# Forgetting attention: transposes of large tiles in a pair of PSUM banks, split by one pass per engine

## The chip, the cores and the metric

The kernel runs on one core of a Trainium2 chip. The metric is the device time of one execution in microseconds (us). Three runs of the kernel before gave 2591.21, 2593.04 and 2594.58 us; the median is 2593.04 us.

Engine names are those of the profile: PE is TensorE, PEld its weight loads, DVE is VectorE, ACT is ScalarE, POOL is GpSimd, SP is SyncE. Each engine runs its own instructions in the order of the program and waits on semaphores for the others.

## What is computed

The program is three transformer layers in fp32 over 1024 tokens of width 1024: a first block (two kinds of attention and a mixture of experts), then a layer with forgetting attention, then a layer with windowed attention. The change lies in the forgetting attention alone:

```python
def fox_attention(q, k, v, log_f):                 # 16 heads, head size 64, 1024 tokens
    c = jnp.cumsum(log_f, axis=1)
    ...
    def block(args):                               # one block of 128 queries
        idx, qi, ci = args
        logits = jnp.einsum('bqhd,bkhd->bhqk', qi, k) * scale
        logits = logits + ci[..., :, None] - c_k[..., None, :]
        logits = jnp.where(causal, logits, -jnp.inf)
        p = jax.nn.softmax(logits, axis=-1)
        return jnp.einsum('bhqk,bkhd->bqhd', p.astype(v.dtype), v)
```

## The kernel before

`phase_fox` works through 16 heads. A head has eight tiles of 128 queries, `qt` 0 to 7; tile `qt` looks at `qt + 1` blocks of 128 keys. The order within a head is 7, 0, 6, 1 and then 5, 2, 4, 3, so that a large tile (`qt` 4 to 7, 5 to 8 blocks, at even `i`) and a small one (`qt` 0 to 3, 1 to 4 blocks, at odd `i`) alternate. The generator `unit(h, half, i)` is one tile, 128 in all. It is cut by `yield` into steps; `go.feed` takes every tile that is under way one step further, the oldest first, and then starts the next one. So in one feed stand, in this order: the last step of tile u-3, the second step of tile u-1, the first step of tile u. The order on each engine is the order in which these steps are written.

1. First step: two or four matmuls of queries and keys (L2117, L2118) into `p_s0` or `p_s1`, then DVE adds the mask and the forget terms and takes the row minimum (L2123).
2. Second step: ACT takes the exponential and the row sum (L2131), from SBUF to SBUF.
3. Last step: PE transposes the tile block by block into PSUM (L2148), `split` copies it out on ACT (rounded to the fast fp32 format, the high part, L341) and DVE subtracts this from the PSUM tile (the low part, L342). The matmuls with the values (L2054, L2055) read both parts three feeds later.

PSUM has eight banks of 512 fp32 columns. In this phase `p_s0` has banks 0 and 1, `p_s1` bank 2, `p_pv` banks 3 and 7. The transposes take their banks from `p_tr`, a ring of banks 4, 5 and 6 that is used all over the program: each call of `tile` takes the next bank. A large tile takes two (four blocks in the first, the rest in the second) and has one `split` for each; a small tile takes one.

After every second head, `scaled(j)` (L2075) makes the factors that normalize a pair of heads: DVE takes the reciprocal of the row sums (L2078), PE transposes it (L2081), ACT copies it out (L315 through `acopy`), and it goes through DRAM (`d_ra`) to all partitions. It is started when the pair's last tile, `qt` 3, takes its second step. Its PE transpose is written right behind the transposes of that `qt` 3 tile and takes the next bank of `p_tr`. A wait is made for whoever last read or wrote the bank's place.

Of the kernel before, what the change touches and what calls it, by code (L numbers as in the profile page):

```python
# [19 lines left out]
P = 128  # L20
# [45 lines left out]
def f(ap):  # L66
    return ap.bitcast(F32)
# [226 lines left out]
def three_layer_kernel(ctx: ExitStack, tc: tile.TileContext, I, out, stop=99, dbg=None):  # L294
    nc = tc.nc
    V, A, G, T, SP = (GUARD(e) for e in (nc.vector, nc.scalar, nc.gpsimd, nc.tensor, nc.sync))
    ctx.enter_context(tc.manual_schedule())
    sb = Arena(ctx.enter_context(tc.tile_pool(name="sbuf", bufs=1)), SLOTS, SMALL)
    banks = Banks(ctx.enter_context(tc.tile_pool(name="psum", bufs=1, space=PSUM)).tile([P, 4096], F32, name="ps"))
    p_mm = banks.ring([0], [1], [2], [3])  # L300
    p_s = banks.ring([0, 1], [2, 3])
    p_tr = banks.ring([4], [5], [6])
# [34 lines left out]
    def split(hi, lo, src, scale=None, e=V):  # L337

        if scale is None:
            if e is V:  # L340
                A.activation(out=hi, in_=src, func=AF.Copy)  # L341
                e.tensor_tensor(lo, src, f(hi), op=OP.subtract)  # L342
            else:
                e.tensor_copy(hi, src)
                for k in range(src.shape[1]):
                    fine(lo[:, k], src[:, k], f(hi[:, k]), OP.subtract)
        else:
            A.activation(out=hi, in_=src, func=AF.Copy, scale=scale)
            V.scalar_tensor_tensor(lo, src, scale, f(hi), op0=OP.mult, op1=OP.subtract)
# [1664 lines left out]
    def phase_fox(og, wo, last):  # L2014

        p_s0, p_s1, p_pv = banks.ring([0, 1]), banks.ring([2]), banks.ring([3], [7])
        fc, pp, ptp, sm = Rings(sb), Rings(sb, 2), Rings(sb, 2), Rings(sb, 4)
        CS, cs = {}, fc.tile([P, 10 * P], F32, name="cs")

        def masked(h, qt):  # L2020


            c = FX[h][2]
            n = (qt + 1) * P
            if qt > 3:
                d = slice(qt * P, n)
                G.affine_select(out=c[:, d], in_=c[:, d], compare_op=OP.is_ge, fill=-BIG, base=0, pattern=[[-1, P]],
                                channel_multiplier=1)
                CS[qt] = c[:, :n]
            else:  # L2030
                CS[qt] = cs[:, qt * (qt + 1) // 2 * P:][:, :n]
                G.affine_select(out=CS[qt], in_=c[:, :n], compare_op=OP.is_ge, fill=-BIG, base=qt * P,
                                pattern=[[-1, n]], channel_multiplier=1)

        pp.reserve_pairs("sb", 2)
        pp.reserve_pairs("pt", 4)
        RS, PT, ended, late = {}, {}, set(), []
        todo = Todo(FDELAY)


        ORDER = ((7, 0, 6, 1), (5, 2, 4, 3))

        def pv_chunks(h, top, hi, lo):

            v = FX[h][3]
            box = {}

            def chunk(k0, k1):
                if k0 == 0:
                    box["ps"] = p_pv.tile([P, 256], name="pv")  # L2050
                ps = box["ps"]
                for kt in range(k0, k1):
                    q0 = P if kt == top else 0
                    T.matmul(ps[:, q0:], lhsT=v[:, kt], rhs=hi[:, kt, q0:], start=(kt == 0), stop=False)  # L2054
                    T.matmul(ps[:, q0:], lhsT=v[:, kt], rhs=lo[:, kt, q0:], start=False, stop=(kt == top))  # L2055
                if k1 == top + 1:
                    a = h % 2 * 64
                    o = og.at(h // 2, top - 1, 2)[a:a + 64]
                    acopy(o, ps[0:64])
                    late.append((o, ps[64:128], h, top))  # L2060
                    if top == 3:
                        sb.drop(f"fv{h}")

            for k0 in range(0, top + 1, 2):
                todo.add(lambda k0=k0: chunk(k0, k0 + 2))

        def add_halves():

            for o, ps, h, top in late:
                V.tensor_tensor(o, o, ps, op=OP.add)  # L2070
                if top == 3:
                    ended.add(h)
            late.clear()

        def scaled(j):  # L2075

            r = RS.pop(j)
            V.reciprocal(r, r)  # L2078
            yield
            ps = p_tr.tile([P, 4, P], name="rtr")[0:16, 0]  # L2080
            T.transpose(ps, r.rearrange("p a t -> p (a t)"), ident)  # L2081
            rt = sm.tile([16, P], F32, name="rt")
            acopy(rt, ps)
            yield
            yield
            SP.dma_start(out=d_ra[2 * j:2 * j + 2].rearrange("a (t p) -> (a t) p", p=P), in_=rt)
            yield
            yield
            rr = pp.tile([P, S], F32, name="rr")
            for a in range(2):  # L2090
                bc_load(rr[a * 64:(a + 1) * 64], d_ra[2 * j + a], S)
            yield
            yield
            while 2 * j + 1 not in ended:
                yield
            for th in range(2):
                o = og.at(j, 4 * th, 4)
                fine(o, o, rr[:, th * 512:(th + 1) * 512], OP.mult)

        def unit(h, half, i):  # L2100
            todo.step()
            qt = ORDER[half][i]
            if half == 0 and i == 0:
                if h % 2 == 0:
                    RS[h // 2] = sm.tile([P, 2, NT], F32, name="rs")
            if half == 0 and i == 3:
                fox_load(h + 1)
            if half == 1 and i == 2:
                fox_load_v(h + 1)
            q, k, c = FX[h][:3]  # L2110
            qs = slice(qt * P, (qt + 1) * P)
            n = (qt + 1) * P
            todo.some(FTAKE)
            ps = (p_s1 if i % 2 else p_s0).tile([P, 512 if i % 2 else S], name="s")
            for c0 in range(0, n, 512):
                w = min(512, n - c0)
                T.matmul(ps[:, c0:c0 + w], lhsT=q[:, qs], rhs=k[:, 0, c0:c0 + w], start=True, stop=False)  # L2117
                T.matmul(ps[:, c0:c0 + w], lhsT=q[:, qs], rhs=k[:, 1, c0:c0 + w], start=False, stop=True)  # L2118
            nm = sm.tile([P, 1], F32, name="nm")
            sbt = pp.tile([P, S], F32, name="sb")  # L2120
            pt = pp.tile([P, S], F32, name="pt", bufs=4)

            V.tensor_tensor_reduce(sbt[:, :n], ps[:, :n], CS[qt], -1.0, 3e38, OP.add, OP.min, nm)  # L2123
            add_halves()
            if half == 1 and i == 3:
                sb.drop(f"fq{h}", f"fk{h}", f"fc{h}")
            u = 8 * h + 4 * half + i + 2
            if u < 128:
                masked(u // 8, ORDER[u // 4 % 2][u % 4])
            yield  # L2130
            A.activation(out=pt[:, :n], in_=sbt[:, :n], func=AF.Exp, scale=-1.0, bias=nm,  # L2131
                         accum_out=RS[h // 2][:, h % 2, qt:qt + 1])
            if half == 1 and i == 3 and h % 2:
                go.spawn(scaled(h // 2))
            yield
            yield
            kind = i % 2
            if i < 2:
                nb = (8, 4)[kind]
                PT[h, half, kind] = (ptp.tile([P, nb, 256], F32R, name=f"phi{kind}"),  # L2140
                                     ptp.tile([P, nb, 256], F32R, name=f"plo{kind}"))
            hi, lo = PT[h, half, kind]
            cs = slice((qt % 2) * P, (qt % 2 + 1) * P)
            for b in range(0, qt + 1, 4):
                m = min(4, qt + 1 - b)
                tr = p_tr.tile([P, 4, P], name="ptr")
                for j in range(m):
                    T.transpose(tr[:, j], pt[:, (b + j) * P:(b + j + 1) * P], ident)  # L2148
                split(hi[:, b:b + m, cs], lo[:, b:b + m, cs], tr[:, :m])
            if i >= 2:  # L2150
                pv_chunks(h, qt | 1, hi, lo)

        masked(0, 7)
        masked(0, 0)
        for h in range(16):
            for half in range(2):
                for i in range(4):
                    wo.step(WO_FOX.get(8 * h + 4 * half + i, ()))
                    go.feed(unit(h, half, i))
        last()  # L2160
        n = 0
        while go.active or go.fresh or not todo.empty():
            todo.step()
            todo.some(3)
            go.feed()
            add_halves()
            if n == 0:
                pp.drop("sb")
            if n == 2:
                pp.drop("pt")  # L2170
            wo.step(WO_FOX.get(128 + n, ()))
            n += 1
        for r in (fc, pp, ptp, sm):
            r.close()
# [345 lines left out]
```

## Time and profile before

| | |
|---|---|
| median of three runs | 2593.04 us |
| the profiled execution's own time | 2593.18 us |
| span of its profile, first to last instruction | 2591.4 us |
| PE / DVE / ACT busy over the span | 94% / 70% / 56% |
| forgetting attention | about 1780 to 2024 us of the span |
| mean granted TensorE clock | 0.973 of full speed |

A busy share over the whole span mixes stages with different limits; for this change only the stretch of the forgetting attention counts. A matmul's end is modelled in the profile, and matmuls overlap, so that consecutive ones start closer together than each one takes. In a timeline row stand the start in us from the span's start, the duration, engine, line, operation, tiles, size and count; the bracket at its end is the idle time of the engine before it and what ended it.

### The profile page before, as it was taken

Reading aid. Unit: us, or ns where it says so; the run is one execution under the profiler, and the core shown is the slowest. Engines: PE = TensorE matmul, PEld = TensorE weight load, DVE = VectorE, ACT = ScalarE, POOL = GpSimd, SP = SyncE. Lnnn points to the kernel's source line nnn. Section 1 sums busy time; section 2 is a strip of 40 time slices with the busy share of each in tenths; the row PEclk is TensorE's granted clock in tenths of the full one; section 3 lists DMA queues with packets and bytes.
Section 4 is the critical chain, followed back from the end, with each engine's and each line's share of the span. In section 5 each row is a group of like instructions: output and inputs, shape, how many; then the busy total and the mean of one; then the engine's idle time right before and its main releaser. Section 6 shows DMA issues by size and latency. Waiting matters only on the chain. (4 is left out here: it accounts for less than half of the span.)

```text
span 2591.4 us, 36430 instructions
## 1 busy us (share of the span) xinstructions
PE 2424.8 (94%) x12998; PEld 1987.6 (77%) x12998; DVE 1825.9 (70%) x3051; ACT 1439.2 (56%) x2513; POOL 648.8 (25%) x714
## 2 busy tenths in 40 slices
PE   5999899998988999999996999999999899999989
PEld 3889788887876777777765978787888689787867
DVE  7654588887667999999998445535998546655952
ACT  3324577777216888888874434324888334424940
POOL 0000089936001222222211022201234102210340
PEclk9999999999988999999998999999999899999989
DMA  7346765553748999999978544336776436336833
GB/s 266 116 130 174 226 190 166 172 172 119 254 176 275 385 390 387 384 378 381 382 280 283 174 127 122 113 103 176 192 211 193 148 110 181 108 110 168 228 104 124
DMA packets 300237, 542.70 MB, mean 209 GB/s; under 512 B 45307, under 2 KB 206331, under 8 KB 273430
## 3 DMA queue, kind: packets, MB, share of 16 engines
q1 hardware_dynamic: 292886, 523.56, 62.1%
q0 software_dynamic: 7168, 16.79, 1.9%
q8 instruction: 104, 1.70, 0.3%
q14 instruction: 79, 0.65, 0.1%
HBM read 434.68 MB, written 113.98 MB: 212 GB/s over the span
## 5 line engine op out<-in xcount | busy, mean ns | idle before, releaser
L365 PE MATMUL ps<-t,t 128*128 128x512 f32 (+4 forms) x8224 | 1761.6, 371 | 20.6 <-ACT t L341 15.6
L365 PEld LDWEIGHTS ps<-t,t 128*128 128x128 f32 (+1 forms) x8224 | 1374.2, 183 | 338.6 <-ACT t L341 17.1
L342 DVE TENSOR_TENSOR t<-t,t 128x2048 fp32r<-128x2048 f32 (+4 forms) x258 | 494.0, 1942 | 57.8 <-ACT t L341 57.5
L341 ACT ACTIVATE t<-t 128x2048 fp32r<-128x2048 f32 (+4 forms) x258 | 420.2, 1632 | 157.6 <-PE ps L365 115.9
L342 DVE TENSOR_TENSOR t<-ps,t 128x512 fp32r<-128x512 f32 (+3 forms) x628 | 371.1, 620 | 56.0 <-ACT t L341 52.8
L341 ACT ACTIVATE t<-ps 128x512 fp32r<-128x512 f32 (+3 forms) x628 | 316.1, 539 | 166.1 <-PE ps L377 70.4
L322 POOL TENSOR_TENSOR small<-small 128x8 f32<-128x8 f32 (+3 forms) x120 | 137.6, 1147 | 899.4 <-DVE small L321 861.9
L335 POOL TENSOR_TENSOR t<-t,t 128x256 f32<-128x256 f32 (+1 forms) x288 | 212.3, 770 | 118.1 <-DMA t<-d_rb 31.0
L317 ACT ACTIVATE t<-ps,small 96x512 f32<-96x512 f32 (+3 forms) x168 | 104.4, 621 | 202.8 <-PE ps L365 200.0
L315 ACT ACTIVATE t<-ps 64x256 f32<-64x256 f32 (+5 forms) x200 | 83.6, 420 | 130.3 <-PE ps L365 69.8
L1572 POOL DMA_INDIRECT d_ye<-t,small x32 | 45.2, 1412 | 437.0 <-ACT t L317 430.3
L2131 ACT ACTIVATE t<-t,small 128x1024 f32<-128x1024 f32 (+7 forms) x128 | 99.1, 775 | 27.4 <-DVE small L2123 24.3
L2123 DVE CUSTOM_DVE_ANT_0 t<-ps,t 128x1024 f32<-128x1024 f32 (+7 forms) x128 | 95.7, 747 | 23.1 <-PE ps L2118 13.2
L377 PE MATMUL ps<-small,t 96*128 96x96 f32 (+1 forms) x608 | 76.3, 264 | 35.0 <-DVE t L1930 18.7
L377 PEld LDWEIGHTS ps<-small,t 96*128 96x128 f32 (+1 forms) x608 | 67.5, 145 | 52.8 <-DVE t L1930 19.1
L453 DVE TENSOR_TENSOR t<-ps,t 128x512 f32<-128x512 f32 x32 | 22.1, 691 | 113.2 <-PE ps L365 102.3
L686 POOL TENSOR_SCALAR t<-t,small 128x1024 f32<-128x1024 f32 x32 | 93.1, 2910 | 32.6 <-DMA t<-in_w_ada_dram 32.6
L2227 DVE TENSOR_TENSOR t<-t,ps 128x512 f32<-128x512 f32 x32 | 22.0, 687 | 110.5 <-PE ps L365 110.5
L1568 POOL DMA_INDIRECT t<-d_h,small x32 | 89.0, 2783 | 37.7 <-DVE small L1276 28.2
L1769 DVE TENSOR_REDUCE small<-t 128x8 f32<-128x512 f32 (+1 forms) x56 | 36.2, 647 | 85.7 <-ACT t L1768 85.5
L2148 PE MATMUL ps<-small,t 128*128 128x128 f32 x576 | 89.3, 282 | 5.8 <-ACT t L2131 3.5
L1150 PE MATMUL ps<-t,t 128*128 128x512 f32 x320 | 83.4, 407 | 7.8 <-ACT t L1196 7.5
(297 smaller groups left out, 2984.5 us busy)
## 6 DMA issues: line engine op xcount, KB each, us to landing
t<-in_w_expert_gate_dram SPq DMA_DIRECT2D x64, 1024.0 KB, 10.7
t<-in_w_expert_up_dram SPq DMA_DIRECT2D x64, 1024.0 KB, 10.8
t<-in_w_expert_down_dram SPq DMA_DIRECT2D x64, 1024.0 KB, 10.1
t<-in_w_ada_dram SPq DMA_DIRECT2D x48, 512.0 KB, 5.1
t<-d_ak SPq DMA_DIRECT2D x64, 256.0 KB, 6.9
t<-in_w_in_a_dram SPq DMA_DIRECT2D x14, 1024.0 KB, 7.7
t<-in_x_dram SPq DMA_DIRECT2D x16, 512.0 KB, 5.2
t<-d_dk SPq DMA_DIRECT2D x16, 512.0 KB, 8.5
```

The lines of the kernel that those rows point to most:

```text
L317: A.activation(out=dst, in_=src, func=AF.Copy, scale=scale)
L322: G.tensor_tensor(dst, dst, mhalf[:, :dst.shape[-1]], op=OP.pow)
L335: G.tensor_tensor(out[:, c:c + 256], a[:, c:c + 256], b[:, c:c + 256], op=op)
L341: A.activation(out=hi, in_=src, func=AF.Copy)
L342: e.tensor_tensor(lo, src, f(hi), op=OP.subtract)
L365: T.matmul(ps, lhsT=a(k), rhs=b(k), start=(first and i == 0), stop=(last and i == n - 1))
L377: T.transpose(ps[:, k], src[:, (c + k) * P:(c + k + 1) * P], ident[:m, :m])
L686: G.tensor_scalar(w, w, cc[:, k:k + 1], None, op0=OP.mult)
L1568: G.indirect_dma_start(out=xg[e % 3], out_offset=None, in_=d_h2, in_offset=rows(idx_in[:CAP, e:e + 1]), bounds_check=S - 1, oob_is_err=False)
L2123: V.tensor_tensor_reduce(sbt[:, :n], ps[:, :n], CS[qt], -1.0, 3e38, OP.add, OP.min, nm)
L2131: A.activation(out=pt[:, :n], in_=sbt[:, :n], func=AF.Exp, scale=-1.0, bias=nm, accum_out=RS[h // 2][:, h % 2, qt:qt + 1])
L2148: T.transpose(tr[:, j], pt[:, (b + j) * P:(b + j + 1) * P], ident)
```

## The change

Within `phase_fox` the transposes no longer use `p_tr`. Large tiles write all their blocks into one tile of two banks, 4 and 5 (`p_t0`), and small tiles into bank 6 (`p_t1`). A tile of either kind is split by one ACT copy and one DVE subtraction over all its blocks; the small tiles had one of each before. The transpose of the reciprocal row sums in `scaled` takes bank 6 as well.

```diff
         p_s0, p_s1, p_pv = banks.ring([0, 1]), banks.ring([2]), banks.ring([3], [7])
+        p_t0, p_t1 = banks.ring([4, 5]), banks.ring([6])
...
-            ps = p_tr.tile([P, 4, P], name="rtr")[0:16, 0]
+            ps = p_t1.tile([P, 4, P], name="rtr")[0:16, 0]
             T.transpose(ps, r.rearrange("p a t -> p (a t)"), ident)
...
-            for b in range(0, qt + 1, 4):
-                m = min(4, qt + 1 - b)
-                tr = p_tr.tile([P, 4, P], name="ptr")
-                for j in range(m):
-                    T.transpose(tr[:, j], pt[:, (b + j) * P:(b + j + 1) * P], ident)
-                split(hi[:, b:b + m, cs], lo[:, b:b + m, cs], tr[:, :m])
+            m = qt + 1
+            tr = p_t1.tile([P, 4, P], name="ptr") if kind else p_t0.tile([P, 8, P], name="ptr")
+            for j in range(m):
+                T.transpose(tr[:, j], pt[:, j * P:(j + 1) * P], ident)
+            split(hi[:, :m, cs], lo[:, :m, cs], tr[:, :m])
```

Lines of the changed kernel behind the new ring are one higher up to L2144 (L2081 is L2082, L2117 is L2118); the transposes stay on L2148.

PE, kernel before, where the third pair of heads begins: the last tile of the head before (`qt` 3, four blocks), the transpose of the reciprocals, the matmuls of the new head's `qt` 6 and the transposes of its `qt` 7.

```order
L2148 MATMUL ps<-small,t_13152 128x128 [waits DVE_49,Activation_49]
L2148 MATMUL ps<-small,t_13152 128x128 x3
L2081 MATMUL ps<-small 16x128 [waits DVE_49]
L2117 MATMUL ps<-t_13740,t_13051 128x512
L2118 MATMUL ps<-t_13740,t_13051 128x512
L2117 MATMUL ps<-t_13740,t_13051 128x384
L2118 MATMUL ps<-t_13740,t_13051 128x384
L2148 MATMUL ps<-small,t_13151 128x128 [waits Activation_49]
L2148 MATMUL ps<-small,t_13151 128x128 x3
L2148 MATMUL ps<-small,t_13151 128x128 [waits DVE_49]
L2148 MATMUL ps<-small,t_13151 128x128 x3
```

The same place on PE in the changed kernel, with the values' matmuls left out, up to the transpose of the next small tile (`qt` 0, one block).

```order
L2148 MATMUL ps<-small,t_13152 128x128 [waits DVE_49,Activation_49]
L2148 MATMUL ps<-small,t_13152 128x128 x3
L2082 MATMUL ps<-small 16x128 [waits DVE_49]
L2118 MATMUL ps<-t_13714,t_13051 128x512
L2119 MATMUL ps<-t_13714,t_13051 128x512
L2118 MATMUL ps<-t_13714,t_13051 128x384
L2119 MATMUL ps<-t_13714,t_13051 128x384
L2148 MATMUL ps<-small,t_13151 128x128 [waits Activation_49]
L2148 MATMUL ps<-small,t_13151 128x128 x7
...
L2148 MATMUL ps<-small,t_13151 128x128 [waits Activation_49]
```

The transposes keep their place; the eight blocks of `qt` 7 have one wait in front instead of two, and the transpose of the reciprocals now stands directly behind four transposes into the same bank 6. The `qt` 0 transpose writes this bank again, and it has no wait for DVE any more: what it would wait for, the subtraction that reads the `qt` 3 tile, is covered by an earlier wait on PE.

DVE, kernel before, at the same place: from the low part of `qt` 4 (two subtractions) over the reciprocal to the low part of `qt` 3.

```order
L342 TENSOR_TENSOR t_13192<-ps,t_13190 128x4x128 [waits Activation_49]
L342 TENSOR_TENSOR t_13192<-ps,t_13190 128x128 [waits Activation_49]
L2078 RECIPROCAL small<-small 128x16
L2123 ISA t_13150,small<-ps,t_13149 128x128 [waits DVE_49,PE_49,Pool_49]
L2123 ISA small 128x1
L2070 TENSOR_TENSOR t_13145<-t_13145,ps 64x256 [waits Activation_49]
L342 TENSOR_TENSOR t_13223<-ps,t_13222 128x4x128 [waits Activation_49]
```

DVE in the changed kernel, the same stretch.

```order
L342 TENSOR_TENSOR t_13192<-ps,t_13190 128x5x128 [waits Activation_49]
L2079 RECIPROCAL small<-small 128x16
L2124 ISA t_13150,small<-ps,t_13149 128x128 [waits DVE_49,PE_49,Pool_49]
L2124 ISA small 128x1
L2071 TENSOR_TENSOR t_13145<-t_13145,ps 64x256 [waits Activation_49]
L342 TENSOR_TENSOR t_13221<-ps,t_13220 128x4x128 [waits Activation_49]
```

The low part of `qt` 4 is one subtraction over five blocks; the rest keeps its order: the reciprocal stands four instructions ahead of the subtraction that reads the `qt` 3 tile.

## Rows read from the trace of the kernel before

**Rows 1.** Windows: the whole forgetting attention, and two neighbouring heads; columns as headed.
```profile
core 0: us, PE busy (x) PEld busy (x) DVE busy (x) ACT busy (x) POOL busy (x), PEclk, DMA share, GB/s
1780.00:2024.00 244.00, 220.52 (x1586) 199.26 (x1587) 212.31 (x519) 205.32 (x518) 78.42 (x174) 0.98 0.75 201
1852.46:1866.45 13.99, 13.46 (x102) 12.34 (x101) 13.22 (x32) 12.57 (x34) 3.81 (x10) 1.00 0.78 194
1866.45:1881.46 15.01, 13.69 (x103) 12.39 (x102) 13.43 (x33) 13.19 (x32) 3.12 (x9) 1.00 0.74 186
```

**Rows 2.** Waits in 1780 to 2024 us: total, times, longest us.
```profile
PE ps L2081 <- DVE small L2078: 10.2, 8, 1.3
```

**Rows 3.** Timeline where a head begins and the reciprocals are transposed.
```profile
1867.34 0.62 PE L2148 MATMUL ps<-small,t 128*128 128x128 f32 x4
...
1867.78 1.15 ACT L2131 ACTIVATE t<-t,small 128x1024 f32<-128x1024 f32 x1
...
1868.96 0.24 DVE L2078 RECIPROCAL small<-small 128x16 f32<-128x16 f32 x1
...
1869.26 0.28 PE L2081 MATMUL ps<-small 128*16 128x128 f32 x1 [1.30 <-DVE small L2078]
...
1869.45 0.60 ACT L341 ACTIVATE t<-ps 128x512 fp32r<-128x512 f32 x1
...
1870.08 0.69 DVE L342 TENSOR_TENSOR t<-ps,t 128x512 fp32r<-128x512 f32 x1 [0.20 <-ACT t L341]
...
1870.20 1.28 PE L2148 MATMUL ps<-small,t 128*128 128x128 f32 x8
```

**Rows 4.** Chain of waits, last TensorE piece before the next head's first DVE instruction.
```profile
1881.09 0.25 PE ps L2118
```

**Rows 5.** Timeline, same head: the tile `qt` 6, then the transposes of `qt` 5.
```profile
1874.25 0.93 PE L2148 MATMUL ps<-small,t 128*128 128x128 f32 x7
...
1874.89 0.98 ACT L341 ACTIVATE t<-ps 128x512 fp32r<-128x512 f32 x2 [0.48 <-PE ps L2148]
...
1876.02 1.16 DVE L342 TENSOR_TENSOR t<-ps,t 128x512 fp32r<-128x512 f32 x2
...
1876.86 0.85 PE L2148 MATMUL ps<-small,t 128*128 128x128 f32 x6
```

**Rows 6.** Timeline, the head before it: the same two tiles.
```profile
1858.96 0.93 PE L2148 MATMUL ps<-small,t 128*128 128x128 f32 x7
...
1859.91 0.95 ACT L341 ACTIVATE t<-ps 128x512 fp32r<-128x512 f32 x2
...
1860.72 1.15 DVE L342 TENSOR_TENSOR t<-ps,t 128x512 fp32r<-128x512 f32 x2
...
1861.83 0.87 PE L2148 MATMUL ps<-small,t 128*128 128x128 f32 x6 [0.28 <-ACT t L2131]
```

**Rows 7.** Groups by form, 1780 to 2024 us: busy, mean ns, idle before.
```profile
L342 DVE TENSOR_TENSOR t<-ps,t 128x512 fp32r<-128x512 f32 x96 | 64.7, 687 | 3.6 <-ACT t L341 2.1
...
L342 DVE TENSOR_TENSOR t<-ps,t 128x256 fp32r<-128x256 f32 x32 | 13.4, 419 | 0.5
```

**Rows 8.** Timeline: two DVE subtractions of one large tile (`qt` 7).
```profile
1857.42 1.28 DVE L342 TENSOR_TENSOR t<-ps,t 128x512 fp32r<-128x512 f32 x2
```

**Rows 9.** Timeline of PE: two waits elsewhere in the program.
```profile
1531.88 0.60 PE L1901 MATMUL ps<-small 128*16 128x128 f32 x4 [2.51 <-DVE t L1902]
...
541.45 0.47 PE L1187 MATMUL ps<-t,t 128*128 128x512 f32 x1 [3.00 <-DMA t<-d_dq]
```

**Rows 10.** Windows of 20 us around those two waits and around Rows 3.
```profile
1526.00:1546.00 20.00, 17.49 (x80) 14.00 (x80) 7.50 (x13) 3.86 (x8) 4.75 (x3) 0.91 0.29 79
...
535.00:555.00 20.00, 16.89 (x111) 15.02 (x110) 15.37 (x25) 13.29 (x29) 7.34 (x6) 1.00 0.78 251
...
1864.00:1884.00 20.00, 18.52 (x136) 16.56 (x134) 17.91 (x44) 17.71 (x44) 5.66 (x13) 1.00 0.75 198
```

**Rows 11.** Timeline at the phase's end: last `qt` 3 subtraction, last transpose of reciprocals.
```profile
2023.39 0.63 DVE L342 TENSOR_TENSOR t<-ps,t 128x512 fp32r<-128x512 f32 x1
...
2023.52 0.28 PE L2081 MATMUL ps<-small 128*16 128x128 f32 x1 [1.11 <-DVE small L2078]
```

## The prediction

> **What bounds the kernel now.** I read the busy shares by window first, since the shares over the whole span mix stages. In the 244 us of the forgetting attention PE is busy 221, DVE 212 and ACT 205 us [rows 1]: three engines near 90% on one loop, each waiting briefly for the others, so the end is set by a chain that passes from engine to engine. The loop repeats every two heads, 14.0 + 15.0 = 29.0 us, although both heads have the same work; in the second PE is idle more. The waits say where: PE stands 10.2 us in total, eight times, up to 1.3 us, before the transpose of the reciprocals [rows 2], once per pair. The timeline of one such place shows the order of things [rows 3]: the four transposes of the old head's `qt` 3 end at 1867.96, the reciprocal at 1869.20, PE goes on at 1869.26, 0.06 us later, the price of a signal from DVE to PE. From there the chain of waits, read forward, names almost only TensorE until the next head's first DVE instruction, its last piece being the query-key matmul at 1881.09 to 1881.34 [rows 4]. So in this head whatever delays that transpose delays the head's end.
>
> **What the change saves.** Each of the 64 large tiles loses one ACT and one DVE instruction. The DVE subtraction takes 687 ns at 512 columns and 419 at 256 [rows 7], 1.05 ns per column and 0.15 us fixed. Two back to back overlap: 1.28 us for the pair [rows 8], against 0.687 + 512 x 1.05 = 1.22 for one of 1024 columns. The saving is 0.06 us, 64 x 0.06 = 3.8 us of DVE, and about as much of ACT. At most this reaches the end, at least nothing. I count no separate gain: the saved time is in the durations that I use below.
>
> The Trainium skill, page "VectorE: DVE Perf Modes", section "The TRN2 errata", puts the fixed cost of one DVE instruction at about 150 cycles measured; that would be an estimated 0.156 us for each instruction left out, 10 us for 64. The trace agrees on the size of the fixed part, but shows that a neighbour hides most of it; the pair's measured 1.28 us decides.
>
> **The transpose of the reciprocals.** Before, it takes the next bank of the ring, and waits for the reciprocal alone. Now it writes bank 6, into which PE has just put the four blocks of `qt` 3. It may not start until ACT has copied these out and DVE has subtracted. The printed order bears this out: the next small tile's transpose into that bank lists no wait for DVE any more, so an earlier one covers it. That subtraction cannot come sooner: ACT is first held by the 1.15 us exponential of the new head's `qt` 7 and an output copy, and copies `qt` 3 only at 1869.45 to 1870.05; DVE subtracts at 1870.08 to 1870.77 [rows 3]. With 0.06 for the signal PE goes on at 1870.83, not 1869.26: +1.57 us. The bounds are 0 (it still goes with the reciprocal) and 1.57; the rows leave nothing in between, and I take 1.57. Queued behind it on PE are the matmuls of `qt` 6, for which DVE waits, and the transposes of `qt` 7; behind the copy of the reciprocals on ACT stands the exponential of `qt` 0, which has slack.
>
> Something goes in exchange. The eight transposes of `qt` 7 took 1.28 us [rows 3]; seven take 0.93 [rows 5] and four 0.62 [rows 3], 0.10 each, so eight take 1.04 to 1.09. The rest was a wait in the middle, for the same `qt` 3 subtraction, whose bank the ring had given to their second half. That wait is now behind: -0.2 us. Net +1.37 per pair.
>
> **The later start of the copy.** ACT could begin after four transposes, now it needs all. Where this matters is `qt` 6 followed by `qt` 5, whose transposes write the same two banks and now wait for one undivided subtraction. In the head with the reciprocals [rows 5], shifted by 1.37: the transposes of `qt` 6 run 1875.62 to 1876.55, the copy of 896 columns (0.91, the pair's 0.98 less 0.07) ends at about 1877.50, the subtraction (1.09) at 1878.62, and with the signal `qt` 5 starts at 1878.68 in place of 1876.86: +1.82, so another 0.45. In the other head [rows 6]: the transposes end at 1859.89, the copy at 1860.83, the subtraction, which before ran beside the second copy from 1860.72 on, from 1860.86 to 1861.95, and `qt` 5 starts at 1862.01 in place of 1861.83: +0.18. The bounds of this term are 0 and 0.63 per pair; the durations are those of the rows, and I take 0.63. For `qt` 7 I count nothing: its subtraction waits behind another DVE instruction anyway, and the copy's end comes before; that cover is some 0.2 us thick. For `qt` 5 and 4 the passes are shorter.
>
> Sum per pair 2.0 us. Seven pairs follow each other: 14.0 us. The eighth transpose of reciprocals, at the phase's end, waits until 2024.02 + 0.06 in place of 2023.52 [rows 11], up to +0.55 on the way to the next layer, at least 0 since ACT and DVE are busy with weights there; I take 0.3.
>
> **The clock of TensorE.** The wait at each pair grows from 1.30 to about 1867.96 to 1870.83 = 2.87 us. The seven waits of 1.30 us leave the clock at full speed (1.00 over the 20 us around one [rows 10]). Longer ones often do not: after the wait of 2.51 us at 1531.88 [rows 9] the mean over 20 us is 0.91 [rows 10], which is 0.09 x 20 = 1.8 us of full-speed time gone; after 3.00 us at 541.45 it stays 1.00. In the trace there are six such waits of 2.0 to 3.0 us standing alone, of which these two are shown; after five the clock fell to its lower level, 1.2 in place of 2.4 GHz. PE has no slack in the 12 us behind the reciprocals, so a fall there costs all of about 1.7 us. Bounds: none to seven falls, 0 to 12 us. By the share seen, 5 of 6, I take five: 8.5 us.
>
> The Trainium skill ("TensorE: Matmul & The Clock Gate", Part 1) states that the clock is at one of two levels and that an idle TensorE is throttled; by that rule the longer wait is what speaks most against this change. The five falls agree with it, the wait of 3.00 us shows an exception.
>
> **The sum.** 2593.2 (profiled execution, 0.14 above the median, so I use it for both) + 14.0 + 0.3 + 8.5 = 2616.0 us.
>
> **Rivals.**
> The bank makes PE wait, but the clock holds: 2593.2 + 14.3 = 2607.5 us, and 2602.8 if only the 1.37 per pair arrives. For it: the 3.00 us wait without a fall. Against: the other five.
>
> The shorter passes win. DVE and ACT together set the pace in the first head of the pair, and if PE's wait at the reciprocals costs less than 3.8 / 7 = 0.5 us per pair, the saving of up to 3.8 us decides: 2589.4 us. For it: DVE busy 13.2 of 14.0 us there [rows 1]. Against: the wait is on PE, in order, and PE's chain behind it has no gap to take it up; and the saving is already spent on the later start of the copy.
>
> Both cancel, or the transpose of the reciprocals does not wait for the subtraction after all: 2593 us. Against: the missing DVE wait in the printed order.
>
> The two banks lock all large tiles: transposes, copy and subtraction in a ring with one buffer. For `qt` 7 that is 1.04 + 1.01 + 1.22 + 0.15 for signals = 3.4 us, against 3.5 to 3.75 us for a large and a small tile (14.0 / 4, 15.0 / 4). It fits by a hair; if the queues in front of ACT and DVE add 0.3 us on the 32 tiles of `qt` 7 and 6, 10 us come on top of the forecast: 2626 us.
>
> **How the numbers follow.** Forecast with falls of the clock: 0.58, its own range 2610 to 2621 us (two to seven falls). Bank wait without falls: 0.27. Locked large tiles: 0.06. Cancelling: 0.05. Faster: 0.04. The range 2602 to 2622 takes in the first two with the bounds of their terms; outside remain the last three, 0.15. A measurement of this kernel can tell 0.2%, 5.2 us, from no change: faster means under 2587.9, slower over 2598.2. The first three cases are slower, 0.91; cancelling is same, 0.05; faster 0.04.
>
> **What would show it.** In the profile after: the wait of PE before the transpose of the reciprocals is about 2.9 us, eight times in all, with the subtraction (L342) as what ended it; a pair of heads takes about 31 us without and 32.7 with a fall; the clock row shows falls behind these waits; in the matmul's waits the large transposes appear as waiting for DVE L342. The copies of large tiles number 64 and take about 1.0 us at 1024 columns. Wrong would be the forecast if the transpose of reciprocals is still released by the reciprocal, if PE's chain behind it has gaps that shrink, or if the seven longer waits leave the clock at 1.00 throughout.

## The result, and the profile after

The changed kernel takes 2615.78 us in the median of four runs (2612.31 to 2619.97), the kernel before 2593.70 us (2591.21 to 2594.58). The ratio is 1.0089, with a 95% interval of 1.0077 to 1.0101: slower by 0.9%. The profiled execution took 2616.51 us, its span is 2614.8 us.

The waits of the forgetting attention name the place. PE waits as often as before for the transpose of the reciprocals (L2082 now), eight times, but seven of these waits are 2.86 us long instead of 1.30 (the eighth, at the phase's end, 1.59 instead of 1.11), and something else ends the wait: VectorE's subtraction L342, not the reciprocal [rows 2]. Columns are total, times and longest wait in us.

```profile
PE ps L2082 <- DVE t L342: 21.6, 8, 2.9
```

The timeline of one such place, the start of the same head as in [rows 3], with start, duration, operation and the idle time before it:

```profile
1868.57 0.62 PE L2148 MATMUL ps<-small,t 128*128 128x128 f32 x4
...
1869.01 1.15 ACT L2132 ACTIVATE t<-t,small 128x1024 f32<-128x1024 f32 x1 [0.17 <-DVE small L2124]
...
1870.13 0.24 DVE L2079 RECIPROCAL small<-small 128x16 f32<-128x16 f32 x1
...
1870.68 0.60 ACT L341 ACTIVATE t<-ps 128x512 fp32r<-128x512 f32 x1
...
1871.31 0.69 DVE L342 TENSOR_TENSOR t<-ps,t 128x512 fp32r<-128x512 f32 x1 [0.20 <-ACT t L341]
...
1872.05 0.28 PE L2082 MATMUL ps<-small 128*16 128x128 f32 x1 [2.86 <-DVE t L342]
...
1872.99 1.79 PE L2148 MATMUL ps<-small,t 128*128 128x128 f32 x8
```

The reciprocal is there at 1870.37, but PE starts 0.05 us after the subtraction has ended, at 1872.00. The eight transposes of `qt` 7 take 1.79 us without a wait inside: here the clock falls (0.60 from 1873.0 to 1873.5). Windows from one transpose of reciprocals to the next (that is one pair of heads) show both parts of the loss side by side. The columns are those of [rows 1].

```profile
1840.86:1872.05 31.19, 26.87 (x201) 24.74 (x201) 26.34 (x57) 25.66 (x57) 8.32 (x20) 1.00 0.72 187
1872.05:1904.79 32.74, 28.46 (x202) 26.31 (x203) 26.34 (x57) 25.74 (x57) 8.35 (x20) 0.93 0.69 178
1904.79:1938.75 33.96, 29.66 (x201) 27.24 (x201) 26.43 (x57) 25.64 (x57) 8.31 (x20) 0.90 0.67 170
```

Before, a pair took 29.0 us [rows 1]. At full clock (1.00) it now takes 31.19, that is 2.19 more; where the clock falls, 32.74 and 33.96. DVE's and ACT's busy time does not move, so they only wait longer. Windows of 20 us around the seven places have clocks of 1.00, 1.00, 0.91, 0.83, 0.83, 0.91 and 0.91; two of them:

```profile
1861.00:1881.00 20.00, 16.57 (x112) 15.24 (x111) 14.63 (x33) 14.68 (x32) 4.02 (x12) 0.91 0.66 163
1892.00:1912.00 20.00, 16.58 (x106) 15.28 (x105) 14.31 (x33) 14.40 (x35) 2.74 (x8) 0.83 0.62 162
```

So the clock fell behind five of seven waits of 2.86 us, behind none of the seven of 1.30 us before (one of them in [rows 10]). The late copies stand in the same head, to be held against [rows 5]:

```profile
1878.38 0.93 PE L2148 MATMUL ps<-small,t 128*128 128x128 f32 x7
...
1879.34 0.92 ACT L341 ACTIVATE t<-ps 128x896 fp32r<-128x896 f32 x1 [0.80 <-PE ps L2148]
...
1880.29 1.09 DVE L342 TENSOR_TENSOR t<-ps,t 128x896 fp32r<-128x896 f32 x1 [0.18 <-ACT t L341]
...
1881.53 0.85 PE L2148 MATMUL ps<-small,t 128*128 128x128 f32 x6 [0.54 <-DVE t L342]
```

ACT idles until the seventh transpose has ended, DVE until the whole copy has, and PE 0.54 us until the subtraction has. Before, the copy started after four transposes, and PE did not wait here.

The transposes of `qt` 7, then `qt` 6 and `qt` 5 of both heads, in the pair of heads from 1840.86 on in which the clock does not fall:

```profile
1841.80 1.04 PE L2148 MATMUL ps<-small,t 128*128 128x128 f32 x8
...
1845.62 0.93 PE L2148 MATMUL ps<-small,t 128*128 128x128 f32 x7
...
1848.80 0.85 PE L2148 MATMUL ps<-small,t 128*128 128x128 f32 x6 [0.59 <-DVE t L342]
...
1859.93 0.93 PE L2148 MATMUL ps<-small,t 128*128 128x128 f32 x7
...
1863.09 0.85 PE L2148 MATMUL ps<-small,t 128*128 128x128 f32 x6 [0.56 <-ACT t L315]
```

From the start of `qt` 6 to that of `qt` 5 it is 3.18 and 3.16 us, against 2.60 and 2.87 at the same places before: 0.58 and 0.29 more. The eight transposes of `qt` 7 take 1.04 us instead of the 1.28 of [rows 3], since there is no wait inside. Together with the longer wait for the reciprocals' place, 1.56 - 0.24 + 0.58 + 0.29 = 2.19 us: the pair's loss at full clock comes apart without a rest. In the second head the profile names an output copy (L315) as what ended the wait, but the subtraction of `qt` 6 ends 0.15 us before the transposes start, as in the first head, and it, not L315, reads the banks that they write.

The single pass itself is as cheap as reckoned: 1024 columns take 1221 ns on DVE, against 1.28 us for the pair of halves [rows 8].

```profile
L342 DVE TENSOR_TENSOR t<-ps,t 128x1024 fp32r<-128x1024 f32 x16 | 19.5, 1221 | 9.8 <-ACT t L341 9.8
...
L341 ACT ACTIVATE t<-ps 128x1024 fp32r<-128x1024 f32 x16 | 16.4, 1025 | 14.5 <-PE ps L2148 13.8
```

### The profile page after: what moved, and what is told of

It is laid out like the page before. It is cut to its first block, busy times and chain, and to the rows that moved or that the text cites. A ratio compares the mean times of both kernels' runs of the same rounds, so it can differ in the third digit from the quotient of the medians.

```text
span 2614.8 us, 36288 instructions
## 1 busy us (share of the span) xinstructions
PE 2422.4 (93%) x12998; PEld 1986.7 (76%) x12998; DVE 1823.2 (70%) x2987; ACT 1438.2 (55%) x2449; POOL 648.7 (25%) x714
## 5 line engine op out<-in xcount | busy, mean ns | idle before, releaser
L342 DVE TENSOR_TENSOR t<-t,t 128x2048 fp32r<-128x2048 f32 (+4 forms) x258 | 493.1, 1938 | 57.4 <-ACT t L341 57.1
L342 DVE TENSOR_TENSOR t<-ps,t 128x512 fp32r<-128x512 f32 (+7 forms) x564 | 366.8, 673 | 69.7 <-ACT t L341 67.2
L341 ACT ACTIVATE t<-ps 128x512 fp32r<-128x512 f32 (+7 forms) x564 | 311.9, 583 | 185.5 <-PE ps L377 69.8
L315 ACT ACTIVATE t<-ps 64x256 f32<-64x256 f32 (+5 forms) x200 | 83.5, 419 | 130.6 <-PE ps L365 69.8
L2148 PE MATMUL ps<-small,t 128*128 128x128 f32 x576 | 89.7, 286 | 14.1 <-DVE t L342 5.3
L453 DVE TENSOR_TENSOR t<-ps,t 128x512 f32<-128x512 f32 x32 | 22.1, 691 | 113.2 <-PE ps L365 102.6
L455 ACT ACTIVATE t<-t 128x512 f32<-128x512 f32 x32 | 20.2, 632 | 125.5 <-DVE t L453 125.5
```

Source lines behind the costliest of these rows:

```text
L2148: T.transpose(tr[:, j], pt[:, j * P:(j + 1) * P], ident)
```

## The experiments

The theory: the loss is the wait on the shared bank 6, the falls of the clock behind it, and, smaller, the late pass (the one copy and one subtraction of a large tile, which start only when all its blocks are transposed). The chief rival: the pair of banks with its one buffer, and the passes over it, hold up all large tiles.

**e1_pair: the change, with the transpose of the reciprocals in the pair of banks.**

```diff
-            ps = p_t1.tile([P, 4, P], name="rtr")[0:16, 0]
+            ps = p_t0.tile([P, 8, P], name="rtr")[0:16, 0]
```

> The changed kernel, with the transpose of the reciprocals in the pair of banks 4 and 5 instead of bank 6. Those are free once the subtraction of the tile of qt 4 has ended, about 0.2 us before the reciprocal. Theory (the shared bank 6 and the clock falls behind it make the loss): TensorE again waits 1.3 us for the reciprocal, the clock stays at full speed behind the seven places, and only the later start of the copies is left, 0.4 to 0.7 us per pair of heads: 2595 to 2599 us. Rival (the large tiles lock in their one buffer): the time stays over 2605 us with the 1.3 us wait. Rival (shorter passes would win without the wait): 2589 us.

Measured: 2599.12 us, 1.0020 of the kernel before (1.0010 to 1.0030). That is just above the range expected. With this one edit some 17 of the 22 us are gone. The wait is short again, and the reciprocal ends it; a pair of heads takes 29.73 us at full clock:

```profile
PE ps L2082 <- DVE small L2079: 9.7, 8, 1.2
```

```profile
1842.02:1871.75 29.73, 27.03 (x202) 24.69 (x202) 26.31 (x58) 25.50 (x58) 8.29 (x20) 1.00 0.77 197
```

The large tiles still share one buffer and one pass, so the locking of all large tiles is not the main cause. What remains is 0.73 us per pair over the 29.0 of [rows 1].

**e2_samebank: the kernel before, with that transpose in the bank of the `qt` 3 tile.**

```diff
+            p_tr.i -= 1
             ps = p_tr.tile([P, 4, P], name="rtr")[0:16, 0]
```

> The kernel before, with one edit: the transpose of the reciprocals goes into the bank of the qt 3 tile just transposed. Rings, passes and copies are those of before. Theory: TensorE waits 2.86 us at each pair, released by the subtraction, +1.37 us per pair, 9.6 us in all, and about five falls of the clock for 8.5 us more: 2611 us (2603 to 2616). Rival (one pass over two banks and the later copy make the loss): no change, 2594 us.

Measured: 2609.94 us, 1.0066 (1.0045 to 1.0088). The bank alone, without any change to the passes, brings most of the loss. The wait is that of the changed kernel:

```profile
PE ps L2082 <- DVE t L342: 21.7, 8, 2.9
```

Two of its pairs, the first with a fall (clock 0.95), the second at full clock up to 1903.4, where the clock falls in the wait at its end (0.98 in the mean):

```profile
1842.31:1873.96 31.65, 28.25 (x201) 25.90 (x201) 26.85 (x65) 25.89 (x65) 8.31 (x20) 0.95 0.73 187
1873.96:1904.38 30.42, 26.91 (x201) 24.75 (x201) 26.75 (x65) 25.67 (x65) 8.32 (x20) 0.98 0.73 190
```

The second takes 30.42 us, another of this kind 30.33: +1.3 to +1.4 over 29.0, beside the +1.37 that the prediction had for the bank alone. In or behind the seven waits the clock fell five times, as in the changed kernel, though not in the same places.

**e3_busy: the change, with 14 transposes of the identity in front of the transpose of the reciprocals,** into the pair of banks; their results are not used.

```diff
+            dm = p_t0.tile([P, 8, P], name="dm")
+            for x in range(14):
+                T.transpose(dm[:, x % 8], ident, ident)
             ps = p_t1.tile([P, 4, P], name="rtr")[0:16, 0]
```

> The changed kernel, with 14 extra transposes of the identity into banks 4 and 5 in front of the transpose of the reciprocals; nothing reads them. They keep TensorE at work during the second half of its wait, which is then cut in two, about 1.1 us idle and 1.5 us of extra transposes; the transpose of the reciprocals still goes only with the qt 3 subtraction. Theory: no fall of the clock behind the first seven places, 31.2 us for every pair, 2593.5 + 7 x 2.2 + 0.5 = 2609 us (2607 to 2611). Rival (what goes beyond 31.2 us per pair is not the clock): 2615 us.

Measured: 2609.72 us, 1.0062 (1.0045 to 1.0080). The wait is cut in two: 1.10 us idle, 1.75 us of transposes, then the transpose of the reciprocals:

```profile
1869.90 0.62 PE L2151 MATMUL ps<-small,t 128*128 128x128 f32 x4
...
1870.74 0.82 DVE L342 TENSOR_TENSOR t<-ps,t 128x640 fp32r<-128x640 f32 x1
...
1871.62 1.75 PE L2083 MATMUL ps<-small 128*128 128x128 f32 x14 [1.10 <-DVE t L342]
1873.39 0.28 PE L2085 MATMUL ps<-small 128*16 128x128 f32 x1
```

From the end of the `qt` 3 transposes to the transpose of the reciprocals it is 2.87 us, as in the changed kernel, so the extra work delays nothing. The clock stays at 1.00 behind all seven places, and a pair takes what it takes in the changed kernel where the clock does not fall:

```profile
1840.43:1871.62 31.19, 28.60 (x215) 26.24 (x216) 26.36 (x58) 25.68 (x58) 8.34 (x20) 1.00 0.72 185
```

This kernel does more work than the changed one and is about 6 us faster in the median (5 to 7 us if each is held against the runs of the kernel before beside it). The pairs show where that comes from: without the falls all of them take 31.2 to 31.3 us, in the changed kernel four take 32.5 to 34.0 us.

**e4_twopass: e1_pair with two passes for each large tile.**

```diff
-            split(hi[:, :m, cs], lo[:, :m, cs], tr[:, :m])
+            for b in range(0, m, 4):
+                e = min(m, b + 4)
+                split(hi[:, b:e, cs], lo[:, b:e, cs], tr[:, b:e])
```

> The kernel of e1_pair (rings of the change, transpose of the reciprocals in the pair of banks), but each large tile is split by two passes per engine again, four blocks and the rest. It tells whether what e1_pair still loses, 0.73 us per pair of heads, comes of the one late pass or of the fixed banks. Theory (late pass): the loss goes and the 0.2 us wait inside the transposes of qt 7 stays away, 28.8 to 29.0 us per pair, 2589 to 2593 us, 5 to 7 us below e1_pair. Rival (banks): 29.7 us per pair, 2597 to 2599 us.

Measured: 2593.87 us, 0.9999 (0.9990 to 1.0009): the time of the kernel before, a shade over the range expected; the runs of the kernel before beside it, 2594.64 in the median, lay higher too.

```profile
1837.06:1865.95 28.89, 27.03 (x202) 24.68 (x203) 26.66 (x66) 25.70 (x66) 8.27 (x20) 1.00 0.77 201
```

Fixed banks cost nothing; the late pass costs 29.73 - 28.89 = 0.84 us per pair, about 6 us in all. Where it costs them shows in the transposes of `qt` 6 and then `qt` 5, first head and second head, here with two passes:

```profile
1841.92 0.93 PE L2148 MATMUL ps<-small,t 128*128 128x128 f32 x7
...
1844.52 0.86 PE L2148 MATMUL ps<-small,t 128*128 128x128 f32 x6
...
1855.61 0.93 PE L2148 MATMUL ps<-small,t 128*128 128x128 f32 x7
...
1858.51 0.87 PE L2148 MATMUL ps<-small,t 128*128 128x128 f32 x6 [0.30 <-ACT t L2132]
```

and in e1_pair with one:

```profile
1846.94 0.93 PE L2148 MATMUL ps<-small,t 128*128 128x128 f32 x7
...
1850.13 0.85 PE L2148 MATMUL ps<-small,t 128*128 128x128 f32 x6 [0.59 <-DVE t L342]
...
1861.26 0.93 PE L2148 MATMUL ps<-small,t 128*128 128x128 f32 x7
...
1864.41 0.84 PE L2148 MATMUL ps<-small,t 128*128 128x128 f32 x6 [0.56 <-ACT t L315]
```

From `qt` 6 to `qt` 5 it is 2.60 and 2.90 us with two passes, 3.19 and 3.15 with one: 0.59 + 0.25 = 0.84.

**e5_slot: the kernel before, with that transpose one feed later and in bank 2.**

```diff
+            if j < 7:
+                yield
-            ps = p_tr.tile([P, 4, P], name="rtr")[0:16, 0]
+            ps = (p_s1 if j < 7 else p_tr).tile([P, 4, P], name="rtr")[0:16, 0]
```

> The kernel before, with the transpose of the reciprocals one feed later (behind the transposes of the new head's qt 7) and in bank 2, which the query-key matmul of qt 0 has left by then; the last pair keeps its place. Theory (the wait at this place is on TensorE's path through the second head): the idle 1.3 us shrinks to about 0.3, TensorE's chain starts about 1 us earlier: 7 x 1.0 = 7 us off, 2586.5 us (2584 to 2590). Rival (VectorE and ScalarE take up the gain, or the next matmuls into bank 2 wait for the copy of the reciprocals): within 2 us of before.

Measured: 2587.26 us, 0.9988 (0.9976 to 0.9999): faster than both kernels, by a little: the interval only just excludes 1. The waits for the reciprocal are gone but for the last, which keeps its place; a pair takes 28.49 us. That is 0.5 us less, where 1.0 was expected.

```profile
1833.97:1862.46 28.49, 27.30 (x203) 24.81 (x202) 26.57 (x66) 25.63 (x65) 8.27 (x20) 1.00 0.79 204
```

```profile
PE ps L2119 <- ACT small L315: 2.5, 7, 0.4
PE ps L2150 <- DVE t L342: 3.8, 15, 0.3
```

Two waits took back part of the gain. The next matmuls into bank 2, those of `qt` 1, wait for ScalarE's copy of the reciprocals once per pair, up to 0.4 us; this is what the rival had named. And the transposes wait for VectorE's subtraction 15 times, 3.8 us, where it was 8 times and 2.0 us in the kernel before.

**e6_slot_after: the change, with the same later place.** The edit is that of e5_slot, with `p_t1` for the last pair.

> The changed kernel with the transpose of the reciprocals one feed later and in bank 2, as in e5_slot. Theory: no wait on the shared bank and no fall of the clock; the late passes remain, 0.6 to 0.7 us per pair over the 28.5 of e5_slot, 29.1 to 29.2 us per pair, 2590 to 2593 us. Rival (the late pass costs only where TensorE was late already): as e5_slot, 2587 us. Rival (other waits of the change remain): over 2598 us.

Measured: 2593.86 us, 0.9997 (0.9987 to 1.0008). The shared bank, its wait and the falls are gone, the late pass remains: 0.72 us per pair more than e5_slot.

```profile
1837.79:1867.00 29.21, 27.20 (x203) 24.79 (x202) 26.20 (x57) 25.52 (x58) 8.30 (x20) 1.00 0.76 200
```

**e7_mixed: e6_slot_after, with one pass for `qt` 4 and 5 and two for `qt` 6 and 7.**

```diff
-            split(hi[:, :m, cs], lo[:, :m, cs], tr[:, :m])
+            w = 4 if qt > 5 else m
+            for b in range(0, m, w):
+                e = min(m, b + w)
+                split(hi[:, b:e, cs], lo[:, b:e, cs], tr[:, b:e])
```

> As e6_slot_after, but only the tiles of qt 4 and 5 are split by one pass, those of qt 6 and 7 by two. Theory: the late pass costs at qt 6 only, so the loss of e6_slot_after goes and 32 instructions are saved on each of two engines: 28.3 to 28.5 us per pair, 2585 to 2588 us, the same as e5_slot within what can be measured. Rival (late passes cost at qt 5 and 4 as well): 2589 us or more.

Measured: 2590.74 us, 0.9985 (0.9975 to 0.9996). Its median lies above the range expected, but so do the runs of before beside it; the ratio is that of e5_slot, and so is the pair:

```profile
1837.80:1866.29 28.49, 27.24 (x203) 24.83 (x202) 26.38 (x62) 25.55 (x62) 8.27 (x20) 1.00 0.78 205
```

So the late pass costs nothing at `qt` 4 and 5; by the rows under e4_twopass its cost lies at `qt` 6. The 32 instructions saved on each of DVE and ACT bring nothing that can be seen: DVE is 0.2 us less busy per pair (26.57 to 26.38), and the pair is as long.

## Why the prediction was right

Forecast were 2616.0 us, measured 2615.78. Term by term:

- *The transpose of the reciprocals waits for the subtraction that reads bank 6.* Shown: L342 ends the wait in the trace, e2_samebank makes the same wait out of the kernel before, e1_pair takes it out of the changed one. The wait was to be 2.87 us and is 2.86.
- *Net +1.37 per pair, since the wait inside the transposes of `qt` 7 goes away.* e2_samebank: +1.3 to +1.4. In the changed kernel the wait grows by 1.56 and the transposes of `qt` 7 lose 0.24. That this exchange exists shows in e4_twopass too, whose 28.89 us per pair is 0.1 under the kernel before, whose ring made the second half of `qt` 7 wait.
- *The later start of the copy, +0.63 per pair.* Too small: 0.84 from e1_pair and e4_twopass. The mechanism is as told, `qt` 6 with `qt` 5 behind it, in both heads: 0.59 and 0.25 where 0.45 and 0.18 were forecast. Most of the miss is the signal. I took 0.06 us from the end of a subtraction to the next matmul, from the transpose of the reciprocals; the transposes of `qt` 5 start 0.15 us after it (1880.29 + 1.09 = 1881.38, start 1881.53), and that comes twice per pair. The rest, some 0.03 us, is within the reading of the rows.
- *2.0 us per pair, 14.0 for seven.* 2.19 at full clock, 15.3. The two edits apart give 1.3 to 1.4 (e2_samebank) and 0.73 (e1_pair), 2.1 together: they nearly add up.
- *The clock falls behind five of seven waits, 8.5 us.* It did fall five times. The share that the forecast went by, 5 of 6, would have given nearer six; five was a choice that came true. Four of them lie in pairs that can be measured, 32.74, 33.96, 33.90 and 32.50 us against 31.19, together 8.3 us; with the fifth it is nearer 10. Two falls lasted twice as long and took 2.7 us each instead of 1.7, the other two 1.3 and 1.55. In the medians, e3_busy against the changed kernel, the falls are worth about 6 us. The two do not quite agree, and why is not shown: each median is of four runs, and only one execution of each kernel was profiled, so how many falls the others had is not known.
- *The saved passes bring nothing of their own.* Right, and e7_mixed shows it for `qt` 4 and 5, where the late copy does not interfere.
- *The end of the phase, +0.3 us.* The wait there grew from 1.11 to 1.59 us, +0.48, inside the bounds of 0 and 0.55; how much of it reached the next layer was not measured by itself. The sign named for the profile, 2.9 us eight times, holds for seven.

The sum of these terms is 22.8 us in the forecast, 22.1 between the medians. In the one profile the pairs and falls make 15.3 and nearly 10, together 25 us, but its span is only 23.4 us longer than that of before: the forgetting attention began at 1774.19 us instead of 1777.54, behind code that is the same. So the closeness of the total is in part luck: two terms were some 1.3 us too small each, and a difference outside the change made up for it in the profile. What made the medians come out at 22.1 is not shown.

The rivals fell: the locked large tiles by e1_pair and e4_twopass; the transpose that does not wait for the subtraction by the trace; the clock that holds by the five falls and e3_busy; the gain by shorter passes by the slower kernel itself and by e7_mixed.

## What to carry to other kernels

A scratch tile inherits the wait of whoever used its bank last: look for the instruction on the in-order engine directly ahead of it, and give it a bank whose reader is done. Where three engines pass a tile on, one long pass on each saves its fixed cost and loses the overlap between its halves; here, at `qt` 6 with `qt` 5 behind it in the same banks, the overlap was worth more. And a wait on TensorE is not worth its length alone, since its clock can fall behind it.

## What was not expected of the hardware

- The price of a wait on TensorE was not in proportion to its length: seven waits of 1.30 us left the clock at 1.00, in or right behind ten of fourteen waits of 2.86 to 2.91 us (the changed kernel and e2_samebank) it fell, and behind the same wait cut into 1.10 us of idling and 1.75 us of useless transposes in none of seven (e3_busy). Lengths between 1.30 and 2.86 us were not tried at this place. Filling a wait with work that nothing reads made the kernel about 6 us faster.
- From the end of VectorE's subtraction to TensorE's next matmul it is 0.05 us before the transpose of the reciprocals and 0.06 before the extra transposes of e3_busy (1870.74 + 0.82 = 1871.56, start 1871.62), but 0.15 before the transposes of `qt` 5. The size of the first weight load does not explain it: it has 16 columns in the first case and 128 in the other two. What does is open.
